# Nearest-neighbour upsampling on one core: two of three loads move behind the opening barrier, the second behind a VectorE memset

## The chip, the core and the metric

The kernel runs on one core of a Trainium2 chip. The core has five engines, each with its own instruction queue: TensorE (PE), VectorE (DVE), ScalarE (ACT), GpSimd (POOL) and SyncE (SP). Transfers between the device memory (HBM) and the on-chip memory (SBUF, 128 partitions) run on 16 DMA engines, which any of the queues can feed by issuing a DMA instruction. The metric is the device time of one execution in microseconds; each kernel is run several times and the median is taken. Beside these runs there is one profiled execution, from which every row of a trace shown here comes.

## The reference

```python
def setup_inputs():
    batch, channels, h, w = (16, 64, 64, 64)
    return {'x': np.random.randn(batch, channels, h, w).astype(np.float32), 'scale_factor': 2}

def reference(x, scale_factor):
    ...
    for i in range(new_h):
        for j in range(new_w):
            result[:, :, i, j] = x[:, :, i // scale_factor, j // scale_factor]
```

Every input element is written four times, as a 2 x 2 block of the output. 16.78 MB are read and 67.11 MB are written; nothing is calculated.

## The kernel before

The input is seen as 65,536 rows of 64 floats. Partition p holds 512 consecutive rows (R = 512), so each partition reads one stretch of 128 KB and writes one stretch of 512 KB. One big SBUF tile, `mem`, holds all input rows (`xt`, at its end) and the space for expanded rows in front of them.

*Loads.* Three DMA instructions on SP's queue (line 197, cut at rows 0, 32, 288 and 512) bring in 32, 256 and 224 rows of each partition: 1 MB, 8 MB and 7 MB. They are called load 1, load 2 and load 3 here. `cuts` and `HEAD` (lines 194 and 195) give the borders.

*The opening barrier.* A program of this kind opens with a barrier of all five engines: each drains its queue and reports, POOL gathers the reports and releases the others, and then each engine branches to the block with the kernel's own instructions. POOL sets four small constants before it reports. `begin_before_barrier` (lines 13 to 33) is run when the program is finished: it takes the first `EARLY` instructions of SP in the kernel's block, which must be DMA instructions without a wait, and puts them in front of SP's drain of the opening barrier. With `EARLY = 3` all three loads are issued before SP reports to the barrier.

*Expansion.* The list `rows` (line 181) cuts the 512 rows into nine pieces of 38 to 64 rows. For each piece VectorE copies the rows with broadcast reading patterns into expanded form (line 217). The first piece is made by two copies: its first row alone (line 216, 128x256), which needs load 1, and the other 53 rows (line 217, 128x13568), which need load 2 too. Later pieces write over expanded rows that have been stored and over input rows that have been expanded, so their copies wait for earlier stores.

*Stores.* Each piece is stored by one DMA instruction (line 219), of 5.0 to 8.4 MB: the first, second and last on SP's queue, the six others on ACT's. A store waits for VectorE's copies. In the trace the transfers of one queue start one behind the other, in the order in which they were issued.

*The end.* `close_early` (lines 80 to 151) arranges the closing barrier so that SP's last instruction waits for the last store. The change does not touch it.

What sets the order around the change is the order of instructions on SP's queue and the waits that the tile framework adds: it makes an instruction wait for the last writer of the bytes that it writes or reads.

Of the kernel before, what the change touches and what calls it, by code (L numbers as in the profile page):

```python
# [6 lines left out]

EARLY = 3  # L10


def begin_before_barrier(nc):
# [5 lines left out]
    sp = mybir.EngineType.SP  # L19
    loads = [i for i in body.instructions if i.engine == sp][:EARLY]  # L20
    for load in loads:
# [132 lines left out]
@with_exitstack  # L154
def kernel(
    ctx: ExitStack,
    tc: tile.TileContext,
    x: bass.AP,
    scale_factor: int,
    out: bass.AP,  # L160
):
    nc = tc.nc
    nc.at_finalize(begin_before_barrier)
    nc.at_finalize(close_early)
    P = nc.NUM_PARTITIONS
    s = int(scale_factor)
    B, C, H, W = x.shape
    R = B * C * H // P
    fdt = x.dtype

    xp = x.rearrange("b c h w -> (b c h) w").rearrange("(p r) w -> p r w", p=P)
    op = out.rearrange("b c (h hd) w -> (b c h) (hd w)", hd=s).rearrange(
        "(p r) w -> p r w", p=P
    )

    rows = [54, 38, 54, 60, 54, 62, 64, 62, 64]
    GROW = s * s
    FREE = 79
    WF = FREE * GROW * W
    assert sum(rows) == R
    mem_pool = ctx.enter_context(tc.tile_pool(name="mem", bufs=1))
    LEAD = 32
    whole = mem_pool.tile([P, LEAD + WF + R * W], fdt, name="mem")
    mem = whole[:, LEAD:]
    xt = mem[:, WF:].rearrange("p (r w) -> p r w", r=R)  # L190

    HEAD = 32
    cuts = [0, HEAD, R // 2 + HEAD, R]
    for lo, hi in zip(cuts, cuts[1:]):
        nc.sync.dma_start(out=xt[:, lo:hi], in_=xp[:, lo:hi])  # L197

    def expanded(r0, r1):
        return (  # L200
            xt[:, r0:r1].unsqueeze(2).unsqueeze(4).to_broadcast([P, r1 - r0, s, W, s])
        )

    r0 = 0
    before = (0, 0)
    for n, k in enumerate(rows):
        size = k * GROW * W
        at = 0 if n % 2 == 0 else WF + r0 * W - size
        assert at >= before[1] or at + size <= before[0]
        before = (at, at + size)  # L210
        u = mem[:, at : at + size].rearrange(
            "p (k a w b) -> p k a w b", k=k, a=s, w=W
        )
        k0 = 1 if n == 0 else 0
        if k0:
            nc.vector.tensor_copy(out=u[:, :k0], in_=expanded(r0, r0 + k0))  # L216
        nc.vector.tensor_copy(out=u[:, k0:], in_=expanded(r0 + k0, r0 + k))  # L217
        issuer = nc.sync if n in (0, 1, len(rows) - 1) else nc.scalar
        issuer.dma_start(out=op[:, r0 : r0 + k, :], in_=u)
        r0 += k  # L220
# [35 lines left out]
```

## Time and profile before

| what | us |
|---|---|
| time, median of 3 runs | 197.05 (197.05 to 197.31) |
| time of the profiled execution | 197.08 |
| its span in the profile | 195.8 |
| VectorE busy | 76.9 |
| first piece's 53-row copy waits for load 2 | 19.0 |
| all later copies wait for stores, in total | 65.6 |

The span runs from the first instruction shown (SP's issue of load 1) to the last. The profiled execution's time is 1.28 us longer than its span; that part lies outside of what the profile shows. In the chain of waits, each row is a piece of the work that ended last, followed back from the end. The view by stretches of time gives for each stretch the busy time of the engines, the busy share of the 16 DMA engines and the rate in GB/s; it books a packet in the stretch in which it starts, so in stretches of a microsecond or less a share can be far over 1, and the stretch behind it empty.

### The profile page before, as it was taken

The numbers are of one execution on the slowest core, as the hardware profiler recorded it, in microseconds if no ns is written. First come the engines' busy times: TensorE is split into PE (matmuls) and PEld (weight loads), VectorE is DVE, ScalarE is ACT, GpSimd is POOL, SyncE is SP. The second block draws the span as 40 slices with busy tenths as digits, with TensorE's granted clock in tenths as the row PEclk, the third lists the DMA queues.
The fourth block names the chain that finished last, engine by engine and source line by source line (L and its number), as shares of the span: only waits on it lengthen the run. The fifth ranks groups of instructions, "written<-read, shape, count | busy, mean of one in ns | idle before, by whom it ended". The sixth has DMA issues, their size and how long they took to land.

```text
span 195.8 us, 76 instructions
## 1 busy us (share of the span) xinstructions
DVE 76.9 (39%) x10; POOL 0.2 (0%) x4
## 2 busy tenths in 40 slices
DVE  0000099990029287059008805920790079000000
POOL 0000000000000000000000000000000000000000
DMA  9999989989898988999999899999999999999994
GB/s 429 429 429 429 402 375 539 398 362 542 362 435 382 551 373 362 542 402 402 402 537 407 362 542 415 415 415 415 429 429 429 429 415 558 473 435 422 429 429 214
DMA packets 1728, 83.89 MB, mean 429 GB/s; under 512 B 192, under 2 KB 192, under 8 KB 192
## 3 DMA queue, kind: packets, MB, share of 16 engines
q10 hardware_dynamic: 864, 46.66, 55.0%
q1 hardware_dynamic: 864, 37.22, 44.2%
HBM read 16.78 MB, written 67.11 MB: 429 GB/s over the span
## 4 chain that ended last, share of the span: by engine, by line
DMA 61%; DVE 24%; SPq 0%; issue 0%
DMA out_dram<-mem 49%; DVE mem L217 24%; DMA mem<-in_x_dram 12%; SPq L197 0%
## 5 line engine op out<-in xcount | busy, mean ns | idle before, releaser
L217 DVE COPY mem<-mem 128x13824 f32<-128x13824 f32 (+5 forms) x9 | 76.6, 8515 | 84.6 <-DMA out_dram<-mem 65.6
L216 DVE COPY mem<-mem 128x256 f32<-128x256 f32 x1 | 0.3, 293 | 4.8 <-DMA mem<-in_x_dram 4.8
L237 POOL MEMSET const-bfloat16-1.0<- 128x1 bf16 x1 | 0.1, 102 | 0.0
L237 POOL MEMSET const-uint8-127<- 128x1 uint8 x1 | 0.1, 101 | 0.0
L237 POOL MEMSET const-float32-0.0<- 128x1 f32 x1 | 0.1, 98 | 0.2 <-issue 0.2
L237 POOL MEMSET const-float32-1.0<- 128x1 f32 x1 | 0.1, 98 | 0.0
## 6 DMA issues: line engine op xcount, KB each, us to landing
out_dram<-mem ACTq DMA_DIRECT2D x2, 7936.0 KB, 31.6
out_dram<-mem ACTq DMA_DIRECT2D x2, 6912.0 KB, 23.7
out_dram<-mem ACTq DMA_DIRECT2D x1, 7680.0 KB, 26.1
mem<-in_x_dram SPq DMA_DIRECT2D x1, 7168.0 KB, 40.2
out_dram<-mem SPq DMA_DIRECT2D x1, 6912.0 KB, 19.0
out_dram<-mem SPq DMA_DIRECT2D x1, 4864.0 KB, 25.2
mem<-in_x_dram SPq DMA_DIRECT2D x1, 1024.0 KB, 4.8
mem<-in_x_dram SPq DMA_DIRECT2D x1, 23.7
```

Source lines behind the costliest of these rows:

```text
L216: nc.vector.tensor_copy(out=u[:, :k0], in_=expanded(r0, r0 + k0))
L217: nc.vector.tensor_copy(out=u[:, k0:], in_=expanded(r0 + k0, r0 + k))
L237: nc = _bacc.Bacc("TRN2", target_bir_lowering=False, num_devices=1)
```

## The change

Two edits. `EARLY` goes from 3 to 1, so that only load 1 stands in front of SP's drain of the opening barrier; loads 2 and 3 stay in the kernel's own block. And before load 2 is issued, VectorE sets the first 16 of load 2's rows in SBUF to zero, a memset of 128x1024 floats. Load 2 writes the same bytes, so the framework makes its issue on SP wait for the memset. Load 3 stands behind load 2 on SP's queue and has no wait of its own. The memset is the first instruction of VectorE in the kernel's block, in front of the copy of line 216; it waits for nothing but the barrier. The 53-row copy now waits on VectorE's own semaphore too. No other engine's instructions change.

```diff
-EARLY = 3
+EARLY = 1
...
     HEAD = 32
     cuts = [0, HEAD, R // 2 + HEAD, R]
+    PAUSE = 16
     for lo, hi in zip(cuts, cuts[1:]):
+        if lo == HEAD:
+            nc.vector.memset(xt[:, lo : lo + PAUSE], 0.0)
         nc.sync.dma_start(out=xt[:, lo:hi], in_=xp[:, lo:hi])
```

## The prediction

> **What bounds the kernel now.** I read the page's head and slices first, to see which resource is full; then the chain of waits, to see how the opening is tied to the end; then short stretches at the start, to see when packets of load 1 and load 2 start.
>
> ```profile
> span 195.8 us, 76 instructions
> ...
> DVE 76.9 (39%) x10; POOL 0.2 (0%) x4
> ...
> DMA  9999989989898988999999899999999999999994
> GB/s 429 429 429 429 402 375 539 398 362 542 362 435 382 551 373 362 542 402 402 402 537 407 362 542 415 415 415 415 429 429 429 429 415 558 473 435 422 429 429 214
> DMA packets 1728, 83.89 MB, mean 429 GB/s; under 512 B 192, under 2 KB 192, under 8 KB 192
> ```
>
> VectorE is busy for 39% of the span, the DMA engines are busy in every slice: 83.89 MB are moved at a mean of 429 GB/s. The kernel is one long transfer, and only an idle or slow stretch of the DMA engines can change its time.
>
> ```profile
> 0.00 0.38 SPq L197
> 0.38 0.05 issue
> 0.43 23.65 DMA mem<-in_x_dram
> 24.09 0.02 issue
> 24.11 14.30 DVE mem L217
> 38.41 0.02 issue
> 38.42 19.01 DMA out_dram<-mem
> ```
>
> The chain of waits (start, length, what) begins with SP's issue of load 1 (0.38 us) and goes through load 2, which is issued at 0.43 and lands at 24.09. Then come the 53-row copy and the first store. Whatever delays load 2 delays this chain by the same amount. But load 2's 23.65 us are mostly queueing behind load 1, as the stretches show:
>
> ```profile
> 0.00:1.02 1.02, 0.00 (x0) 0.20 (x4) 1.00 0.00 0
> 1.02:1.64 0.62, 0.00 (x0) 0.00 (x0) 1.00 1.32 225
> 1.64:2.00 0.36, 0.00 (x0) 0.00 (x0) 1.00 0.37 114
> 2.00:4.03 2.03, 0.00 (x0) 0.00 (x0) 1.00 0.99 420
> 4.03:4.47 0.44, 0.00 (x0) 0.00 (x0) 1.00 5.60 2420
> 4.47:6.40 1.93, 0.29 (x1) 0.00 (x0) 1.00 0.00 0
> 6.40:6.90 0.50, 0.00 (x0) 0.00 (x0) 1.00 4.84 2097
> ```
>
> The last two columns are the DMA engines' share and GB/s, booked where a packet starts. Nothing starts before 1.02. In 1.02 to 1.64 the 16 engines start their first packets of load 1 (225 GB/s x 0.62 us is 140 KB, 17 packets of 8 KB, which is 1 MB in 128 pieces). In 4.03 to 4.47 come 2420 x 0.44 = 1.06 MB: 16 packets of 64 KB, load 2's first on each engine, and a last two of load 1. Nothing starts until 6.40, and then 2097 x 0.50 = 1.05 MB, the next 16. So load 2, issued at 0.43, has its first packets from 4.03 on: it stands in line for about 3 us. From there on nothing is lost:
>
> ```profile
> 4.03:195.37 191.34, 76.93 (x10) 0.00 (x0) 1.00 1.00 433
> ```
>
> With a share of 1.00 at 433 GB/s up to 0.4 us before the end, the end is the start of load 2's packets on the slowest engine (at most 4.47) plus some 190.9 us of full rate. The prediction is therefore about one instant: does load 2 still start at 4.03 to 4.47?
>
> **The change part by part.** *The barrier.* The timeline, and the instructions of line 237 (the opening barrier's) and of line 251 (the block behind it), carry this:
>
> ```profile
> 0.00 1.33 SPq L197 DMA_DIRECT2D mem<-in_x_dram  x3
> ```
>
> ```profile
> L237 POOLq DRAIN  x1: 179/179/179, 0.3 to 0.3; - x1
> ...
> L237 SPq DRAIN  x1: 125/125/125, 1.4 to 1.4; - x1
> L237 SPq EVENT_SEMAPHORE  x1: 17/17/17, 1.7 to 1.7; - x1
> ...
> L237 DVEq EVENT_SEMAPHORE  x1: 21/21/21, 1.7 to 1.7; - x1
> ```
>
> ```profile
> L251 POOLq DRAIN  x1: 41/41/41, 1.7 to 1.7; - x1
> L251 PEldq DRAIN  x1: 8/8/8, 1.8 to 1.8; - x1
> ```
>
> (The three numbers are shortest, median and longest in ns; then first and last start in us.) SP is the last to report: its three issues end at 1.33, its drain starts at 1.4 and everyone is released at 1.7, 0.37 us behind the last issue. With one issue of 0.38 us before it, the release comes at about 0.38 + 0.37 = 0.75, and POOL, whose own drain ends at 0.3 + 0.18, still arrives earlier. The two issues taken out of the front come back behind the barrier; they are moved past no other DMA, since SP's first store comes at 38.42.
>
> *The branch.* POOL and PE reach the next block's drain at 1.7 and 1.8, within 0.15 us of the release. I give VectorE 0.1.
>
> *The memset.* No row of before has one on VectorE. The nearest are its copies:
>
> ```profile
> L217 DVE COPY mem<-mem 128x13568 f32<-128x13568 f32 x1 | 14.3, 14286 | 19.0 <-DMA mem<-in_x_dram 19.0
> ...
> L217 DVE COPY mem<-mem 128x9728 f32<-128x9728 f32 x1 | 5.2, 5226 | 0.0
> L216 DVE COPY mem<-mem 128x256 f32<-128x256 f32 x1 | 0.3, 293 | 4.8 <-DMA mem<-in_x_dram 4.8
> ```
>
> Two rates: 14286 / 13568 = 1.05 ns an element and 5226 / 9728 = 0.54. The small copy, 293 ns for 256, leaves 293 - 256 x 0.54 = 0.16 us fixed. For 1024 elements the bounds are 0.55 us (fast rate, nothing fixed) and 1.24 us (slow rate with the fixed part). I take 1.2, the end that counts against the change. The Trainium skill's page "VectorE: DVE Perf Modes" (Zero memsets can be issued as uint32) says that a memset takes one cycle for each element, whatever the type; with the 0.96 GHz of its Specifications that is an estimate of 1.07 us before the fixed part, against 0.55 by the fast rows, and this sum's issue would come at 1.95 by the page and 1.43 by those rows. No run here shows a memset yet.
>
> *SP's wake-up* behind VectorE is 0.02 us in the chain (38.41 to 38.42). So load 2 is issued at 0.75 + 0.1 + 1.2 + 0.02 = about 2.1 us instead of 0.43, bounded by 1.4 and 2.2.
>
> *From issue to packets.* Load 1 took 1.02 us to its first packet and 1.64 to the first on the last engine. That gives load 2's first packets at 3.1 to 3.7. The upper bound is the first store, issued at 38.42, whose packets start behind load 3's:
>
> ```profile
> 40.30:40.77 0.47, 0.47 (x1) 0.00 (x0) 1.00 4.36 1883
> ```
>
> 1883 x 0.47 is 885 KB, 16 packets of 54 KB, so it needed no more than 40.30 - 38.42 = 1.9 us to the first and 2.35 to the last. With these, load 2 could start at 4.0 to 4.45. The lower end lies 0.8 to 0.9 us ahead of the engines' need at 4.03 to 4.47, the upper end just meets it. I take load 1's lag, which is a measured lag and not a queue's. Cost: 0. The cover is load 1's own transfer, 3.0 us long; if it were gone, all of the 2.1 - 0.43 = 1.7 us would show.
>
> *What is queued behind.* Load 3 is next on SP and is issued some 0.45 us after load 2 (three issues in 1.33); it is needed when load 2's packets end, 8.4 MB at 433 GB/s or some 19 us after they start. Behind it on SP stands the first store, which is not ready before 38.4. On VectorE the 128x256 copy stands behind the memset and starts at 4.83 in the trace; the memset is done by 2.1. Cost of all three: 0. The extra wait of the 53-row copy, on a memset long done, is a semaphore instruction: 17 to 21 ns for such ones in the rows above, on VectorE, which then waits 65.6 us for stores in total; it could shift only the first store's issue, which is hidden behind load 3.
>
> Sum: 195.8 of span + 0, + 1.28 outside it = 197.08 in the profiled execution's terms, 0.03 above the median of 197.05. I forecast **197.1**.
>
> **The rivals.** *Faster: the opening gets shorter.* From 1.64 to 2.00 load 1's packets start at only 114 GB/s, and load 1 takes 3.0 to 3.4 us from first start to load 2's first, where 1.05 MB at 433 GB/s need 2.42. If the hold-up is the issuing of loads 2 and 3 at the same time (0.43 to 1.33, and their lag), the change takes it away. The slowest engine could then end load 1 at 1.64 + 2.42 = 4.06 instead of 4.47: 0.4 us less, 196.65; the whole ramp gone, from 1.02, would be 1.0, 196.05. For it: the slow stretch coincides. Against it: nine later issues leave the share at 1.00 between 4.03 and 195.37, and load 1 is the only transfer here that starts on idle engines, so its slow first packets can be its own doing.
>
> *Slower: load 2 comes too late and ramps up itself.* The place is the DMA engines' queue at 4.0 to 4.5. If load 2 needs the same ramp as load 1 (to 2.00, up to 1.0 us behind its first start) and its descriptors come when load 1 is already read, the ramp is paid twice: 0.6 to 1.0 us, 197.7 to 198.1. It decides from an issue at 4.47 - 1.64 - 0.7 = about 2.1, if 0.7 us of ramp must be hidden, and from 2.8 if only the lag counts. For it: 2.1 is just what I get. Against it: the store behind load 3 at 40.30 shows no gap. The Trainium skill's page "DMA: Bandwidth & Descriptors" (Rules for kernel authors) advises issuing a DMA early so that its fixed setup cost overlaps, which speaks against moving an issue back by 1.7 us; if none of that overlapped, its rule would give 197.1 + 1.7 = 198.8.
>
> *The change doesn't bring the barrier forward* (something else than SP's issues sets it, release still at 1.7). Load 2 is issued at 3.0, its first packets at 4.05 to 4.65: up to 0.2 us lost, 197.3, still no change.
>
> **How the numbers follow.** A measurement of this kernel can tell 0.2%, 0.4 us, from no change. Forecast 0.38; unmoved barrier 0.05, with the same sign; faster 0.26; slower 0.31. So faster 0.26, same 0.43, slower 0.31. The forecast alone spans 196.8 to 197.4. The range takes in most of both rivals, 196.4 to 198.1; what is left out is a ramp that vanishes and a delay that shows in full.
>
> **What would show it.** In the changed profile: the release at 0.7 to 0.8; the memset from 0.85 to 2.05 (1.2 us, at most 1.24); load 2's issue at about 2.1, load 3's at 2.5. Right: 16 packets of 64 KB start at 4.0 to 4.5 with no empty gap ahead of them, and the 53-row copy starts at about 24.1. Slower: these packets, and the copy, come later by the same amount as the span grows. Faster: the stretch up to 2.0 us carries more than before and the copy starts before 23.8. It would be wrong altogether if the time changes while load 2's packets start where they did.

## The result and the profile after

| | before | after |
|---|---|---|
| median, us | 197.05 (197.03 to 197.31, 6 runs) | 197.88 (197.65 to 198.19, 6 runs) |
| profiled execution, us | 197.08 | 197.9 |
| its span, us | 195.8 | 196.6 |

The ratio after to before is 1.0037, 95% interval 1.0027 to 1.0048. The change makes the kernel slower by 0.83 us at the medians. The 0.8 us are in the span.

The timeline of after (start, length, instructions; in brackets the idle time before and what ended it):

```profile
0.00 2.81 SPq L200 DMA_DIRECT2D mem<-in_x_dram  x3
...
1.07 0.91 DVE L199 MEMSET mem<- 128x1024 f32 x1 [1.07 <-PEq L240]
4.80 0.29 DVE L219 COPY mem<-mem 128x256 f32<-128x256 f32 x1 [2.82 <-DMA mem<-in_x_dram]
24.76 19.55 DVE L220 COPY mem<-mem 128x13568 f32<-128x13568 f32 x2 [19.67 <-DMA mem<-in_x_dram]
39.08 128.52 SPq L222 DMA_DIRECT2D out_dram<-mem  x3
```

and its chain of waits:

```profile
1.07 0.92 DVE mem L199
1.99 0.02 issue
2.00 22.66 DMA mem<-in_x_dram
24.66 0.03 issue
24.69 0.02 DVEq L220
24.71 0.05 issue
24.76 14.30 DVE mem L220
```

The chain now begins with the memset: load 2 is issued at 2.00 instead of 0.43. It lands at 24.66 instead of 24.09, only 0.57 us later for an issue 1.57 us later. Another 0.1 us passes before the 53-row copy starts (0.03 before a second wait instruction, 0.02 for it, 0.05 behind it), where before had 0.02.

Where the 0.57 us arise is in the stretches of after (length, busy times, granted clock, then the DMA engines' share and GB/s; a packet counts where it starts):

```profile
3.99:4.47 0.48, 0.00 (x0) 0.00 (x0) 1.00 5.47 2253
4.47:6.50 2.03, 0.29 (x1) 0.00 (x0) 1.00 0.00 0
6.50:7.10 0.60, 0.00 (x0) 0.00 (x0) 1.00 3.78 1638
7.10:7.44 0.34, 0.00 (x0) 0.00 (x0) 1.00 0.00 0
7.44:7.46 0.02, 0.00 (x0) 0.00 (x0) 1.00 7.56 3277
...
38.80:39.14 0.34, 0.30 (x2) 0.00 (x0) 1.00 0.00 0
39.14:39.16 0.02, 0.02 (x1) 0.00 (x0) 1.00 7.68 2867
39.16:40.30 1.14, 1.14 (x1) 0.00 (x0) 1.00 0.00 0
40.30:40.95 0.65, 0.65 (x1) 0.00 (x0) 1.00 2.99 1276
40.95:41.60 0.65, 0.65 (x1) 0.00 (x0) 1.00 0.00 0
41.60:41.63 0.03, 0.03 (x1) 0.00 (x0) 1.00 4.27 1843
192.40:193.20 0.80, 0.00 (x0) 0.00 (x0) 1.00 2.83 1229
193.20:193.78 0.58, 0.00 (x0) 0.00 (x0) 1.00 0.00 0
193.78:193.80 0.02, 0.00 (x0) 0.00 (x0) 1.00 7.56 3277
```

Load 2's first packets start between 3.99 and 4.47 on all 16 engines, as before. But the second packets do not follow together. 1638 x 0.60 = 983 KB are 15 packets of 64 KB by 7.10, and the sixteenth starts alone at 7.45 (3277 x 0.02 = 66 KB). At 433 / 16 = 27.1 GB/s an engine needs 2.42 us for 64 KB. The late engine's first packet, begun by 4.47, took at least 2.97: it started on time and ran slow, by about 0.55 us. On average the first packets are hardly slow: the share of 5.47 over 0.48 us on 16 engines is 42.0 us of packets, and without the last four 8 KB packets of load 1 (some 1.2 us) 2.55 us are left for each of the 16.

That engine very likely stays last (the rows do not name engines, but one packet is alone behind the others each time). Behind its packet at 7.45 come six more of 64 KB and seven of 56 KB (57,344 bytes, 2.12 us), 7 x 2.42 + 7 x 2.12 = 31.8 us, which leads to 39.2; one packet starts alone at 39.15. It is the last of load 3, and it is slow again: the next, of the first store, starts at 41.60 to 41.63, 2.46 us later instead of 2.12. At the end one packet of 64 KB starts at 193.79 while the 15 others have started by 193.20. In the kernel before the same rows are tight:

```profile
6.40:6.97 0.57, 0.00 (x0) 0.00 (x0) 1.00 4.24 1840
38.10:38.60 0.50, 0.47 (x2) 0.00 (x0) 1.00 4.25 1835
...
192.40:193.00 0.60, 0.00 (x0) 0.00 (x0) 1.00 4.03 1748
193.00:195.30 2.30, 0.00 (x0) 0.00 (x0) 1.00 0.00 0
```

There all 16 second packets start by 6.97 (1840 x 0.57 = 1.05 MB), all of load 3's last by 38.60, and all last packets of the kernel by 193.00. So the loss of 0.8 us is that of the last engine: about 0.55 at the start of load 2 and about 0.3 at the end of load 3. Every engine carries the same bytes, so the slowest one sets the end.

### The profile page after: what moved, and what is told of

It reads as the page before. It is cut to its first block, busy times and chain, and to the rows that moved or that the text cites. A ratio compares the mean times of both kernels' runs of the same rounds, so it can differ in the third digit from the quotient of the medians.

```text
span 196.6 us, 78 instructions
## 1 busy us (share of the span) xinstructions
DVE 77.8 (40%) x11; POOL 0.2 (0%) x4
## 3 DMA queue, kind: packets, MB, share of 16 engines
q1 hardware_dynamic: 864, 37.22, 44.1%
## 4 chain that ended last, share of the span: by engine, by line
DMA 60%; DVE 24%; issue 0%; DVEq 0%
DMA out_dram<-mem 49%; DVE mem L220 24%; DMA mem<-in_x_dram 12%; DVE mem L199 0%; DVEq L220 0%
## 5 line engine op out<-in xcount | busy, mean ns | idle before, releaser
L199 DVE MEMSET mem<- 128x1024 f32 x1 | 0.9, 912 | 1.1 <-PEq L240 1.1
```

Of the source, the lines that this page charges most:

```text
L199: nc.vector.memset(xt[:, lo : lo + PAUSE], 0.0)
```

## The experiments

All ratios are to the kernel before on the same chip, with the 95% interval. "Lands" is load 2's landing in the profiled execution; before has 24.09 and after 24.66.

| run | load 2 issued | lands | median, us | ratio |
|---|---|---|---|---|
| e1, no memset | 0.79 | 24.18 | 197.11 | 0.9999 (0.9990 to 1.0007) |
| e11, 2 rows | 1.07 | 24.12 | 197.15 | 1.0005 (0.9995 to 1.0015) |
| e5, 8 rows | 1.47 | 25.46 | 198.31 | 1.0057 (1.0044 to 1.0070) |
| the change, 16 rows | 2.00 | 24.66 | 197.88 | 1.0037 (1.0027 to 1.0048) |
| e6, 24 rows | 2.54 | 24.32 | 197.29 | 1.0008 (0.9999 to 1.0017) |
| e4, 48 rows | 4.14 | 25.87 | 198.83 | 1.0083 (1.0069 to 1.0097) |

### One part at a time: e1, e2, e3, and the far end: e4

e1 keeps `EARLY = 1` and drops the memset:

```diff
-        if lo == HEAD:
-            nc.vector.memset(xt[:, lo : lo + PAUSE], 0.0)
```

> The change without the memset: load 2 behind the barrier only, issued at about 0.9 us (the change: 2.00). Theory L (load 2's descriptors need a lead of well over a microsecond before its packets start at 4.0 to 4.5, or its first packets are slow on some engines): lead 1.1 us longer, no slow first packets, 197.0 to 197.2. Rival M (the memset itself, its place or its write, costs the time): also 197.0 to 197.2. Rival T (what hurts is load 3 being issued so late that its descriptors arrive as load 2 starts): load 3 issued at 1.35, also 197.0 to 197.2. Rival B (any load behind the barrier costs): 197.6 to 198.0.

Measured: 197.11, ratio 0.9999. Moving two loads behind the barrier costs nothing by itself; rival B falls.

e2 is the kernel before (`EARLY = 3`) with a memset of the same size on bytes of the output space:

```diff
+    nc.vector.memset(mem[:, 0 : 16 * W], 0.0)
```

> The kernel before with the same memset on VectorE, but on bytes of the output space, so that no load waits for it; all three loads ahead of the barrier. Theory L, T, B: as before, 197.0 to 197.2. Rival M: as the change, 197.7 to 198.0.

Measured: 197.18, ratio 1.0000 (0.9991 to 1.0009). The memset as an instruction costs nothing. Writing on load 2's own bytes is not tested by this run, but e6 below writes more of them than the change and loses less, and e5 and e12 write equally many (8 rows) and land load 2 0.8 us apart.

e3 issues loads 1 and 2 early and makes load 3 wait:

```diff
-EARLY = 1
+EARLY = 2
...
-        if lo == HEAD:
+        if lo == cuts[2]:
```

> Loads 1 and 2 ahead of the barrier, load 3 behind a memset of sixteen of its own rows (issued at about 2.3 us). Theory L: load 2's lead is that of before, so 197.0 to 197.2. Rival T: load 3's descriptors arrive while load 2's first packets start, 197.6 to 198.0. Rival B: 197.6 to 198.0.

Measured: 197.11, ratio 0.9997 (0.9989 to 1.0006), with load 3 issued at 2.48. This issue of load 3 is late against that of before (0.9), but not against its own turn, which comes only when load 2's eight packets are through, at about 4.0 + 8 x 2.42 = 23.4. What costs must lie with load 2.

e4 lays a longer memset over the border of loads 2 and 3, so that both wait and stay in order:

```diff
-    PAUSE = 16
+    PAUSE = 24
...
-            nc.vector.memset(xt[:, lo : lo + PAUSE], 0.0)
+            nc.vector.memset(xt[:, cuts[2] - PAUSE : cuts[2] + PAUSE], 0.0)
```

> As the change, with a memset of 48 rows that lie half in load 2 and half in load 3, some 2.7 to 3.3 us long, so that load 2 is issued at 3.8 to 4.4 us and its descriptors come after load 1 has been read. Theory L, and every theory in which the time is an idle stretch: the engines run dry, packets of load 2 start at 5.0 to 6.0 instead of 4.0 to 4.5, and the ramp is paid a second time: 198.6 to 199.8. Rival M: the memset's length counts only through its writes, 198.2 to 199.0 with load 2's packets still starting by 4.5.

Measured: 198.83, ratio 1.0083. The stretches of e4:

```profile
3.90:4.06 0.16, 0.16 (x1) 0.00 (x0) 1.00 0.98 412
4.06:5.09 1.03, 0.34 (x2) 0.00 (x0) 1.00 0.01 0
5.09:6.00 0.91, 0.00 (x0) 0.00 (x0) 1.00 3.36 1152
7.50:8.70 1.20, 0.00 (x0) 0.00 (x0) 1.00 2.02 874
```

The last eight 8 KB packets of load 1 start by 4.06 (412 x 0.16 = 66 KB); at 27.1 GB/s such a packet takes 0.30 us, so load 1 has been read by about 4.36. No data packet starts from there to 5.09. Then load 2's 16 first packets come (1152 x 0.91 = 1.05 MB), and all second ones only after 7.50. This is the plain late case: the engines run dry for some 0.7 us, and the first packets are slow besides, 3.36 x 0.91 = 3.06 us each on average instead of 2.42. Because load 2 meets empty engines here, e4 also shows its lag from issue to packets: 5.09 - 4.14 = 0.95 us to the first and at most 1.86 to the last.

### The dose: e5, e6, e11

The only edit is the number of rows, `PAUSE = 8`, `24` and `2`.

> The change with a memset of 8 rows instead of 16: load 2 issued at about 1.5 us (no memset 0.79 and no loss, 16 rows 2.00 and 0.8 us lost, 48 rows 4.14 and 1.7 lost). Theory L with a threshold (load 2's issue must lie some 2.5 us or more ahead of the instant at which its packets have to start): 197.0 to 197.3, no or few slow first packets. Rival G (loss grows evenly with the lateness of the issue, about 0.4 us a microsecond): 197.4 to 197.5.

> The change with a memset of 24 rows, load 2 issued at 2.4 to 2.6 us. Theory L: more engines with slow first packets, some packets start after 4.5, 198.0 to 198.5. Rival G: 198.0 to 198.2. Rival P (something peculiar to an issue at 2.0, such as two events falling together): back to 197.2 or less.

> The change with a memset of 2 rows, load 2 issued at about 1.05 us, between no memset (0.79, no loss) and 8 rows (1.47, 1.2 us lost). Rival S with a window that opens between them: either 197.0 to 197.3 (the window opens after 1.05) or 198.0 to 198.6 (before it). A loss that falls evenly with lateness from a sharp edge gives 198.4 or more here.

Measured: 198.31 for 8 rows, 197.29 for 24 and 197.15 for 2. An earlier issue (1.47) costs more than the change, a later one (2.54) much less. Theory L, as a threshold on the lead, is wrong, and so is an even growth (rival G), and none of the three forecasts for e6 has its time: it lies above P's 197.2 and far below 198.0. The bad window opens between 1.07 and 1.47, and not at a sharp edge: of e11's eleven runs ten took 197.03 to 197.27 and one 198.20, about e5's time. Stretches of e5 and then of e6:

```profile
3.90:4.60 0.70, 0.00 (x0) 0.00 (x0) 1.00 4.14 1381
4.33:4.64 0.31, 0.00 (x0) 0.00 (x0) 1.00 2.52 846
4.64:5.02 0.38, 0.06 (x1) 0.00 (x0) 1.00 0.00 0
5.02:5.06 0.04, 0.04 (x1) 0.00 (x0) 1.00 4.91 1638
6.40:6.97 0.57, 0.00 (x0) 0.00 (x0) 1.00 0.00 0
6.97:7.50 0.53, 0.00 (x0) 0.00 (x0) 1.00 2.67 1113
7.50:8.70 1.20, 0.00 (x0) 0.00 (x0) 1.00 0.91 382
```

```profile
3.90:4.60 0.70, 0.00 (x0) 0.00 (x0) 1.00 3.94 1580
6.40:6.97 0.57, 0.00 (x0) 0.00 (x0) 1.00 3.18 1380
6.97:7.50 0.53, 0.00 (x0) 0.00 (x0) 1.00 1.14 495
```

In e5 14 first packets start by 4.60 (1381 x 0.70 = 967 KB, with six of 8 KB), yet not one second packet starts before 6.97: all 16 engines run slow, 9 of the second packets come by 7.50 (1113 x 0.53 = 590 KB) and 7 later. The last engine is also late. Its first packet starts alone at about 5.04 (1638 x 0.04 = 66 KB), where before had all 16 by 4.47, and takes 4.91 x 0.04 x 16 = 3.14 us, to 8.18. In 4.33 to 4.64 only 64 KB packets can have started (846 x 0.31 = 262 KB, four of them), so load 1 had been read by about 4.63 and this engine stood empty for 0.4 us or more, although load 2 had been issued 0.53 us sooner than in the change. Of the 1.3 us by which the last second packet is behind that of before (8.18 against 6.88), 0.6 are the late start and 0.7 the slow packet.

In e6 12 second packets have started by 6.97 (1380 x 0.57 = 787 KB) and four follow. The first packets are not faster there than in the change: 3.94 x 0.70 x 16 = 44.1 us, less 2.2 for seven 8 KB packets of load 1, gives 2.62 us each on average, against 2.55. So theory L was right that more packets would be slow and wrong on the time. Only the engine that ends last counts, and in e6 the slow packets did not put one engine far behind the others.

### More cover: e7, e8

e7 is the change and e8 the kernel before, each with load 1 of 64 rows and the second cut kept at 288:

```diff
-    HEAD = 32
-    cuts = [0, HEAD, R // 2 + HEAD, R]
+    HEAD = 64
+    cuts = [0, HEAD, R // 2 + 32, R]
```

> The change with load 1 of 64 rows instead of 32 and load 2 smaller by the same rows: load 2 is issued at 2.00 as in the change, but load 1 now covers until about 6.4. Theory L: the lead is 4.4 us, the loss against the same cut without the change (e8) vanishes, ratio 0.999 to 1.001. Rival B (any load behind a memset and the barrier costs, whatever the cover): still 0.6 to 0.9 us over e8.

> The kernel before with load 1 of 64 rows, all three loads ahead of the barrier: the partner of e7. Every theory: within 0.3 us of before, 196.9 to 197.4, since the DMA engines are busy without a gap either way.

Measured: 198.40 for both; ratios 1.0062 (1.0049 to 1.0074) and 1.0063 (1.0051 to 1.0076). With 4.4 us of lead the change costs nothing, as expected, and its trace agrees. All 16 second packets of load 2 (56 KB here) start together:

```profile
8.60:8.90 0.30, 0.30 (x1) 0.00 (x0) 1.00 7.05 3058
```

But e8 itself was expected at no more than 197.4, and that failed: this cut loses 1.3 us in another place. The whole first piece now lies in load 1, so the first store is issued at 21.83, some 18 us before the engines come to it in the kernel before (40.30). Stretches of e8:

```profile
38.00:40.60 2.60, 0.00 (x0) 0.00 (x0) 1.00 1.29 353
40.60:41.50 0.90, 0.00 (x0) 0.00 (x0) 1.00 0.00 0
41.50:42.50 1.00, 0.00 (x0) 0.00 (x0) 1.00 2.05 885
```

Load 3's 16 last packets (353 x 2.60 = 918 KB) start after 38.00, and the store's first 16 (885 KB) not before 41.50, where the kernel before has them in 40.30 to 40.77 behind a store issued at 38.42. Again it is packets that run slow: 1.29 x 2.60 x 16 = 53.7 us for 16 packets are 3.35 us each, where 56 KB need 2.12.

### Load 3 as the cause, and the queue as the cause: e9, e10, e12

e9 and e10 are the change and e5 with load 3 held back by a second memset:

```diff
+        if lo == cuts[2]:
+            nc.vector.memset(xt[:, lo : lo + 48], 0.0)
```

> The change, with load 3 held back too by a second memset of 48 of its own rows, so that it is issued at about 5.4 us instead of 2.39; load 2 still at 2.00. Theory L fell: a later issue of load 2 (2.55, 197.29) lost less than earlier ones (1.47, 198.31; 2.00, 197.88). Theory T2 (load 3's issue right behind load 2's, while load 2 has not started, is what makes load 2's first packets slow): no slow first packets, 197.0 to 197.3. Rival S (the instant of load 2's own issue against load 1's transfer decides): still 8 or so engines with slow first packets, 197.6 to 198.2.

> The 8-row memset with load 3 held back in the same way (issued at about 4.9 us); load 2 at 1.47. Theory T2: the slow first packets of all 16 engines go, 197.0 to 197.3. Rival S: they stay, 198.0 to 198.6.

Measured: 197.85 (197.48 to 198.96), ratio 1.0037 (1.0024 to 1.0050), and 198.24, ratio 1.0052 (1.0039 to 1.0066). With load 3 issued at 5.22 and 4.70 the losses are those of the change and of e5, and no run of either is within T2's 197.3: theory T2 falls. What is left is load 2's own issue. How much an issue at 2.0 costs varies from one execution to the next: e9's seven runs spread over 1.5 us, and the profiled one is the longest.

e12 moves loads 2 and 3 to ScalarE's queue, with a memset of 16 rows half in each:

```diff
+        loader = nc.scalar if lo else nc.sync
-        nc.sync.dma_start(out=xt[:, lo:hi], in_=xp[:, lo:hi])
+        loader.dma_start(out=xt[:, lo:hi], in_=xp[:, lo:hi])
```

> The change with loads 2 and 3 issued by ScalarE's queue instead of SP's, behind a memset of the same 16-row length (half in load 2, half in load 3), so load 2 is issued at about the same 2.0 to 2.4 us but on another queue than load 1. Theory Q (the slow first packets come from appending to the queue that is just carrying load 1): load 2's packets run at full rate from their start, no 64 KB packet over 2.45 us before 10 us. Rival H (they come from how late the reads of load 2 can begin, on any queue): first packets of 2.5 to 3.3 us on several engines, as in the change. The time also holds the meeting of load 3 with the first store, which now stand on different queues, so it is judged by the packets: 197.0 to 197.6 by Q, 197.5 to 198.6 by H.

Measured: 198.39, ratio 1.0071 (1.0058 to 1.0085), load 2 issued at 2.01 and landed at 24.67. Stretches of e12:

```profile
6.40:6.97 0.57, 0.00 (x0) 0.00 (x0) 1.00 3.72 1610
6.97:7.50 0.53, 0.00 (x0) 0.00 (x0) 1.00 0.57 247
```

14 of the second packets come by 6.97 (1610 x 0.57 = 918 KB) and two later, so first packets were slow here as well, and load 2 lands 0.01 us from where the change has it. It is not the appending to SP's queue that makes them slow: rival H. Only 8 of the memset's rows are load 2's here, as in e5, where load 2 was issued at 1.47 and landed at 25.46. So in these traces the landing goes with the instant of the issue and not with how many of load 2's bytes were written. The further 0.5 us of this run arise after load 2's landing and were not followed up; the first store and load 3 stand on different queues there.

## Why the prediction was right and wrong

The measured 197.88 is 0.8 us above the forecast and outside the 196.8 to 197.4 that the forecast alone spans. It lies in the stated range only because that took in the slower rival, whose mechanism the runs do not bear out for the change. That the number fell inside is luck.

*The bound and the tie to the end: right.* The engines stay busy from load 2's first packets on, and the end follows the slowest engine's progress. That all hangs on one instant, the start of load 2's packets, was wrong (below).

*The barrier: right.* Predicted release 0.75; in after SP and VectorE are released at 0.7 (instructions of the opening barrier, times in ns, then start in us):

```profile
L240 SPq EVENT_SEMAPHORE  x1: 17/17/17, 0.7 to 0.7; - x1
...
L240 DVEq EVENT_SEMAPHORE  x1: 21/21/21, 0.7 to 0.7; - x1
```

The rival in which the barrier does not come earlier is out.

*The memset: right in its end.* Predicted 0.85 to 2.05, measured 1.07 to 1.99. Its row says 0.91 us, less than the predicted 1.2, but it starts later than predicted. e4's memset of 3072 elements shows how these rows are to be read:

```profile
1.49 2.62 DVE L199 MEMSET mem<- 128x3072 f32 x1 [1.49 <-PEq L240]
```

Behind the same barrier it ends at 4.11, 2.13 us after that of 1024 elements: 1.04 ns for each further element. That agrees with an estimate of 1.04 ns from the Trainium skill's page "VectorE: DVE Perf Modes", which has one cycle for each element (Zero memsets can be issued as uint32) and a clock of 0.96 GHz (Specifications). The rows' lengths alone, 2.62 and 0.91, would give 0.83 ns.

*Load 2's issue: right.* 2.1 predicted, 2.00 measured; load 3 at 2.39 instead of 2.5. (With 1.24 for the memset the sum gives 2.1 as its upper bound and not 2.2; the issues of 1.95 and 1.43 come to 1.94 and 1.42.)

*From issue to packets, and the cost of 0: this step failed.* The packets did start at 4.0 to 4.5 with no gap ahead of them, exactly as forecast. For an issue at 2.0 the lag was right too: e4 has 0.95 to 1.86 us where the step took load 1's 1.02 to 1.64. But the step took the start of a packet for its progress, and put the cost at 0. The first packet of the last engine ran 0.55 us slow, the same engine, as far as the rows tell, lost some 0.3 more at the end of load 3, and the end hangs on it: 0.8 us. The prediction named this outcome as the one that would make it wrong altogether: the time changes while load 2's packets start where they did.

*What is queued behind: nearly right.* Load 3 and the 128x256 copy cost nothing (e3; the copy starts at 4.80). The extra wait of the 53-row copy put 0.1 us between landing and copy, where 17 to 21 ns had been reckoned; the first store is issued later by this. At the end it is worth nothing: e11 has the same wait, issues the first store at 38.53 instead of 38.42, and takes the time of before. Not foreseen at all was the second slow packet of the late engine at the end of load 3, about 0.3 us.

*The rivals.* The slower one had the place right (the engines' queue at 4.0 to 4.5), the price right (197.7 to 198.1 against 197.88) and the deciding issue at about 2.1. Its mechanism, that a load issued too late pays its ramp, is shown by e4, where load 2 really comes late. For the change it does not hold: its own sign, that load 2's packets come later, is absent; at 2.54 it would have to cost more than at 2.00, and it costs less; at 1.47 it should cost nothing, and it costs more. The faster rival is out by the change itself: no DMA is issued from 0.38 to 2.00, and load 1 still hands over at 3.99 to 4.47. The advice to issue a DMA early, which the Trainium skill's page "DMA: Bandwidth & Descriptors" gives under Rules for kernel authors, had the sign right for the change: issues at 0.43, 0.79 and 1.07 are free. It does not order the others, since 1.47 costs more than 2.54.

*What stays open* is why load 2's first packets run slow, and why an issue at about 1.5 us makes all of them slow and some late. It is tied to load 2's own issue and repeats in two kernels (e5 and e10), and needs no issue of load 3 right behind it. For the issue at 2.0 the loss vanishes when load 1 covers longer (e7) and does not need the same queue (e12). In every late run load 2 was held back by a memset; no run holds it back by other means. The second slow packet, at the end of load 3, is not explained. An issue at 1.47 falls into the time in which load 1 itself is getting up to speed (up to 2.0 us in the stretches of before), but no run shows by what the one slows the other.

## What to carry to other kernels

A packet that starts on time can still run slow: check when the second packets start, on all engines, before an edit at a hand-over between transfers is costed at nothing. Where each engine has an equal fixed share of the bytes, a slow packet on the engine that ends last is paid in full. To keep a hand-over free here the next transfer had to be issued about 3 us ahead of its turn (by 1.07 for a turn at 4.0, and even so one run of e11 in eleven was slow).

## What was not expected of the hardware

The cost against the instant of issue is not monotonic: nothing up to 1.07, 1.2 us at 1.47, 0.8 at 2.00, 0.2 at 2.54 (its interval reaches down to no change) and 1.7 at 4.14, all against before. And a later issue can start sooner: load 2's last engine got its first packet at 5.04 for an issue at 1.47, and by 4.47 for one at 2.00. Issuing early is not always free: the first store of e8, issued some 18 us ahead of its turn instead of 1.9, comes with a hand-over from load 3 that is some 1.2 us longer. Its cut of the loads differs from that of before too, so the early issue as the cause is only argued.
